# Two steps' results in one 8 MB store, with q and k transposed in place (rotary embedding and q·k scores, float32)

## The chip, the cores and the metric

One core of a Trainium2 chip. The metric is the device time of one execution in microseconds, the median of several runs. Each group of runs stood beside fresh runs of the kernel before on the same chip; the groups were on different chips, so small differences between groups are rough. DVE is VectorE, ACT ScalarE, PE TensorE; SP is the engine whose queue issues nearly all DMA transfers. A transfer is cut into packets, which 16 DMA engines carry: a 4 MB store is 128 packets of 32 KB, eight for each engine. It has landed when its completion is signalled. The *span* is the time of the profiled execution.

## The reference

```python
# q, k: (16, 512, 16, 64) float32; cos, sin: (512, 32)
q_rot = concat([q1*cos - q2*sin, q1*sin + q2*cos])     # k the same
scores = einsum('bshd,bthd->bsht', q_rot, k_rot)       # (16, 512, 16, 512) float32
```

Inputs are 67 MB, the result 268 MB. So the kernel lives from its DMA queue.

## The kernel before

A batch of 512 rows is four *steps* of 128 rows; there are 64 steps. In each one VectorE rotates q and k, TensorE transposes them (into PSUM) and multiplies, ScalarE copies the scores from PSUM into a stage tile of 32 KB per partition, and SP stores the tile. The parts that matter, abridged:

```python
kt_pool = tile_pool(name="kt", bufs=2);  qt_pool = tile_pool(name="qt", bufs=2)   # transposed copies
stage_pool = tile_pool(name="stage", bufs=3)                                      # 3 x 32 KB per partition
o_v = out.rearrange("b (p c) h t -> b c p h t", c=C)
...
def load(which, b):                       # a batch of q or k: 2 MB in one DMA
    ...
def store(i, st):                         # one step: 4 MB
    if i < NST - 1:
        nc.sync.dma_start(o_v[i // C, i % C], st)
        return
    h = H - 2                             # the last step: 14 heads on all DMA engines,
    nc.sync.dma_start(o[:, :h], st[:, :h])
    nc.sync.dma_start(o[:116, h:], st[:116, h:])   # two heads in a split
    nc.sync.dma_start(o[116:, h:], st[116:, h:])
...
# batch 0 (steps 0 to 3) stores 1 MB at a time; k of batch 3 is loaded after step 3
# steps 4 to 63: scores, store(i), rotation and transposes for later steps, loads
```

## Time and profile before

| | before |
|---|---|
| time | 800.53 us (3 runs); 800.99 with a fourth |
| busy: PE, ACT, DVE | 87%, 70%, 68% |
| data queue | 98.6% of the span |
| moved | 335.55 MB on this queue, 336.17 MB on all; 421 GB/s over the span |

The profile is read from the DMA row down. A queue that is full nearly all the time is the bound, and the waits of engines matter only if they leave it empty. Its lines are in the prediction below.

### The profile page before, as it was taken

What the parts mean: (1) busy time and instruction counts of PE and PEld (TensorE: products, weight loads), DVE (VectorE), ACT (ScalarE), POOL (GpSimd) and SP (SyncE); (2) the same over time, 40 slices, a digit from 0 to 9 for tenths busy, and PEclk for the clock granted to TensorE, in tenths of its full rate; (3) what the DMA queues carried; (4) which work ended last, traced back from release to release, by engine and by line L of the source; (5) the groups of instructions that cost most, each with busy time, mean ns of one, the idle gap of its engine ahead of it and who ended that gap; (6) DMA issues with size and microseconds to landing.
All of it is one profiled execution on the core that took longest, in us unless ns stands there. A gap on an engine that the chain in (4) does not pass through costs nothing.

```text
span 799.0 us, 7715 instructions
## 1 busy us (share of the span) xinstructions
PE 691.3 (87%) x3072; PEld 299.3 (37%) x3072; DVE 544.6 (68%) x516; ACT 561.2 (70%) x647; POOL 0.7 (0%) x6
## 2 busy tenths in 40 slices
PE   4989998997979979799797997979979799799970
PEld 2444443343434334343343443424434343344420
DVE  6999987676866768577585775857758478585300
ACT  3888886775857758577585775757757677578870
POOL 0000000000000000000000000000000000000000
PEclk9999999898998989889898898988989899899995
DMA  9999999999999999999999999999999999998995
GB/s 355 422 424 424 432 427 433 425 435 427 421 437 426 439 427 430 433 431 430 431 428 433 434 428 429 433 438 420 418 426 434 435 415 418 426 440 375 422 439 231
DMA packets 17844, 336.17 MB, mean 421 GB/s; under 512 B 1808, under 2 KB 3088, under 8 KB 4240
## 3 DMA queue, kind: packets, MB, share of 16 engines
q1 hardware_dynamic: 17520, 335.55, 98.6%
q8 instruction: 24, 0.39, 0.2%
q10 hardware_dynamic: 288, 0.13, 0.1%
q14 instruction: 12, 0.10, 0.0%
HBM read 67.24 MB, written 268.44 MB: 420 GB/s over the span
## 4 chain that ended last, share of the span: by engine, by line
DMA 50%; PE 40%; ACT 4%; DVE 3%; issue 1%; ACTq 0%; SPq 0%; DVEq 0%
DMA out_dram<-st 47%; PE ps L166 30%; PE bank L127 10%; ACT st L173 4%; DMA q_sb<-in_q_dram 2%; DVE part L106 1%; DMA early<-in_k_dram 1%; DVE q_sb L107 0%; DVE k_sb L107 0%; DVE k_sb L111 0%; DVE q_sb L111 0%; DVE early L107 0%; DVE kT_t L142 0%; ACTq L281 0%; DVE early L111 0%
## 5 line engine op out<-in xcount | busy, mean ns | idle before, releaser
L173 ACT COPY st<-ps 128x1024 f32<-128x1024 f32 x512 | 494.7, 1018 | 203.7 <-DMA out_dram<-st 105.6
L166 PE MATMUL ps<-kT_t,qT_t 64*128 64x512 f32 x2048 | 548.9, 654 | 71.0 <-ACT st L173 70.9
L166 PEld LDWEIGHTS ps<-kT_t,qT_t 64*128 64x128 f32 x2048 | 185.0, 197 | 261.7 <-issue 144.6
L142 DVE COPY qT_t<-bank 128x512 f32<-128x512 f32 x118 | 81.6, 691 | 203.8 <-PE bank L127 203.8
L127 PEld LDWEIGHTS bank<-ident,q_sb 128*128 128x128 f32 x480 | 55.6, 152 | 102.5 <-issue 99.1
L127 PE MATMUL bank<-ident,q_sb 128*128 128x128 f32 x480 | 86.9, 308 | 0.9 <-PE ps L166 0.9
L127 PEld LDWEIGHTS bank<-ident,k_sb 128*128 128x128 f32 x480 | 50.5, 141 | 95.4 <-issue 38.7
L127 PE MATMUL bank<-ident,k_sb 128*128 128x128 f32 x480 | 78.7, 287 | 1.6 <-DVE qT_t L142 1.2
L142 ACT COPY kT_t<-bank 128x512 f32<-128x512 f32 x122 | 72.5, 599 | 6.4 <-PE bank L127 6.4
L107 DVE TENSOR_TENSOR q_sb<-q_sb,cos_t 128x1024 f32<-128x1024 f32 x60 | 73.5, 1226 | 2.1
L111 DVE TENSOR_TENSOR k_sb<-k_sb,part 128x1024 f32<-128x1024 f32 x60 | 73.5, 1225 | 2.1
L107 DVE TENSOR_TENSOR k_sb<-k_sb,cos_t 128x1024 f32<-128x1024 f32 x60 | 73.5, 1225 | 2.0
L106 DVE TENSOR_TENSOR part<-q_sb,ss_t 128x1024 f32<-128x1024 f32 x60 | 73.5, 1225 | 2.0
L106 DVE TENSOR_TENSOR part<-k_sb,ss_t 128x1024 f32<-128x1024 f32 x60 | 73.0, 1216 | 0.1
L111 DVE TENSOR_TENSOR q_sb<-q_sb,part 128x1024 f32<-128x1024 f32 x60 | 73.0, 1216 | 0.0
L127 PE MATMUL bank<-ident,early 128*128 128x128 f32 x64 | 10.5, 316 | 12.5 <-DVE early L111 10.6
L127 PEld LDWEIGHTS bank<-ident,early 128*128 128x128 f32 x64 | 8.3, 161 | 17.5 <-issue 13.4
L106 DVE TENSOR_TENSOR part<-early,ss_t 128x1024 f32<-128x1024 f32 x8 | 9.8, 1223 | 5.9 <-DMA early<-in_k_dram 5.8
L111 DVE TENSOR_TENSOR early<-early,part 128x512 f32<-128x512 f32 x16 | 10.3, 687 | 0.2
L107 DVE TENSOR_TENSOR early<-early,cos_t 128x1024 f32<-128x1024 f32 x8 | 9.8, 1225 | 0.3
L142 ACT COPY qT_t<-bank 128x512 f32<-128x512 f32 x10 | 5.7, 617 | 3.2 <-PE bank L127 3.2
L142 DVE COPY kT_t<-bank 128x512 f32<-128x512 f32 x6 | 4.1, 685 | 0.3 <-PE bank L127 0.3
(9 smaller groups left out, 2.8 us busy)
## 6 DMA issues: line engine op xcount, KB each, us to landing
out_dram<-st SPq DMA_DIRECT2D x59, 4096.0 KB, 23.9
k_sb<-in_k_dram SPq DMA_DIRECT2D x15, 2048.0 KB, 26.9
q_sb<-in_q_dram SPq DMA_DIRECT2D x15, 2048.0 KB, 29.9
out_dram<-st SPq DMA_DIRECT2D x16, 1024.0 KB, 14.3
out_dram<-st SPq DMA_DIRECT2D x1, 3584.0 KB, 20.4
early<-in_k_dram SPq DMA_DIRECT2D x1, 1536.0 KB, 8.9
early<-in_q_dram SPq DMA_DIRECT2D x1, 1536.0 KB, 12.1
early<-in_k_dram SPq DMA_DIRECT2D x1, 512.0 KB
```

What stands on the lines that cost most here:

```text
L106: nc.vector.tensor_tensor(pv, xs, ss, op=mult)
L107: nc.vector.tensor_tensor(xc, xc, cs, op=mult)
L111: nc.vector.tensor_tensor(y, y, z, op=add)
L127: nc.tensor.transpose(bank[:, x, :], src, ident)
L142: copy(out=dst, in_=src)
L166: nc.tensor.matmul(out=po, lhsT=lhs[64 * r : 64 * r + 64, :], rhs=rh, start=True, stop=True)
L173: nc.scalar.copy(out=so, in_=si)
```

## The change

The transposed blocks are written back over their source in the input tiles, so the tiles for transposed q and k go. The memory makes two stage tiles of 64 KB per partition, each for two steps, whose result goes out in one store of 8 MB with 64 KB of contiguous memory per partition. q is loaded in 1 MB pieces, k of batch 2 is loaded at the very start instead of in step 0, and k of batch 3 moves from the end of step 3 into step 2.

```diff
-    kt_pool = ctx.enter_context(tc.tile_pool(name="kt", bufs=2))
-    qt_pool = ctx.enter_context(tc.tile_pool(name="qt", bufs=2))
-    stage_pool = ctx.enter_context(tc.tile_pool(name="stage", bufs=3))
+    stage_pool = ctx.enter_context(tc.tile_pool(name="stage", bufs=2))
...
+    tile_a, tile_b = new_pair(), new_pair()          # [P, 2, H, S]
+    halves = {0: tile_a[:, 0], 1: tile_a[:, 1], 2: tile_b[:, 0], 3: tile_a[:, 0]}
+    def store(i, st):
+        b, c = divmod(i, C)
+        if i == NST - 1:
+            last(o_v[b, :, c], st)
+        elif i == NST - 2:
+            nc.sync.dma_start(o_v[b, :, c], st)
+        elif i % 2 == 1:
+            nc.sync.dma_start(o_v[b, :, c - 1 : c + 1], pairs[i // 2])
...
+    SLOTS = {"k": C, "q": QS}                        # QS = 2: q in 1 MB loads
+    BUFS = {"k": 3, "q": 3}
...
-        copy(out=dst, in_=src)
+        copy(out=x, in_=bank)                        # transposed in place
...
-            if i % C == C - 2:
-                load("q", i // C + 2)
-            elif i % C == C - 1:
-                load("k", i // C + 3)
+            store(i, st)
+            if (i + 1) % QS == 0:
+                load("q", i // QS + BUFS["q"])
+            if c == C - 1:
+                load("k", b + BUFS["k"])
```

More of the change, by code (lines that the diff above doesn't have):

```diff
@@ L31 @@
     G = H // C
+    QS = C // 2
     const_pool = ctx.enter_context(tc.tile_pool(name="const", bufs=1))
@@ L46 @@
     }
-    o_v = out.rearrange("b (p c) h t -> b c p h t", c=C)
+    o_v = out.rearrange("b (p c) h t -> b p c h t", c=C)
     ident = const_pool.tile([P, P], fp32, name="ident")
@@ L53, with last, new_pair, stage @@
     ss_v = ss_t.rearrange("p c x j -> p c (x j)")
-    st_first = [stage_pool.tile([P, H, S], fp32, tag="stage", name="st") for _ in range(2)]
-    early = stage_pool.tile([P, 2 * C * H * D], fp32, tag="stage", name="early")
+    def last(o, st):
+        h = H - 2
+        nc.sync.dma_start(o[:, :h], st[:, :h])
+        nc.sync.dma_start(o[:116, h:], st[:116, h:])
+        nc.sync.dma_start(o[116:, h:], st[116:, h:])
+    def new_pair():
+        return stage_pool.tile([P, 2, H, S], fp32, tag="stage", name="st")
+    tile_a, tile_b = new_pair(), new_pair()
+    pairs = {C // 2: tile_b}
+    halves = {0: tile_a[:, 0], 1: tile_a[:, 1], 2: tile_b[:, 0], 3: tile_a[:, 0]}
+    def stage(i):
+        if i < C:
+            return halves[i]
+        if i // 2 not in pairs:
+            pairs[i // 2] = new_pair()
+        return pairs[i // 2][:, i % 2]
+    def store(i, st):
[6 more added lines that the diff above has]
+            nc.sync.dma_start(o_v[b, :, c - 1 : c + 1], pairs[i // 2])
+    early = tile_b[:, 1].rearrange("p h t -> p (h t)")
     units = {}
@@ L69, in load_units, with load, rope @@
             units[which, (head + h) // G] = t[:, :, D * h : D * (h + G)]
-    batches = {}
-    def load(which, b):
+    tiles = {}
+    SLOTS = {"k": C, "q": QS}
+    BUFS = {"k": 3, "q": 3}
+    def load(which, m):
+        n = SLOTS[which]
+        b, c = divmod(m * n, C)
         if b >= B:
             return
-        t = in_pool.tile([P, C, H * D], fp32, tag=which + "_in", name=which + "_sb")
-        batches[which, b] = t
-        nc.sync.dma_start(t.rearrange("p c (h d) -> p c h d", h=H), dram[which][b])
-    def rope(which, n):
+        t = in_pool.tile(
+            [P, n, H * D], fp32, tag=which + "_in", bufs=BUFS[which], name=which + "_sb"
+        )
+        for x in range(n):
+            tiles[which, m * n + x] = t, x
+        nc.sync.dma_start(
+            t.rearrange("p c (h d) -> p c h d", h=H), dram[which][b, :, c : c + n]
+        )
+    def rope(which, n, count=1):
         part = part_pool.tile([P, H * D], fp32, tag="part", name="part")
@@ L86, in rope @@
             x = units[which, n]
-            sv, k1, k2 = "p c (g j) -> p c g j", {"j": HD}, {"j": D}
+            part = part[:, : H * D]
             cs = cos_t.unsqueeze(2).to_broadcast((P, C, 2 * G, HD))
             ss = ss_v.unsqueeze(2).to_broadcast((P, C, G, D))
-            pv = part.rearrange("p (c g j) -> p c g j", c=C, j=D)
             x5 = x.rearrange("p c (h x j) -> p c h x j", x=2, j=HD)
@@ L93, in rope @@
             adds = [(x5[:, :, :, y], p5[:, :, :, 1 - y]) for y in range(2)]
+            nc_ = C
         else:
-            x = batches[which, n // C][:, n % C]
-            sv, k1, k2 = "p (g j) -> p g j", {"j": HD}, {"j": D}
-            cs = cos_t[:, n % C].unsqueeze(1).to_broadcast((P, 2 * H, HD))
-            ss = ss_v[:, n % C].unsqueeze(1).to_broadcast((P, H, D))
-            pv = part.rearrange(sv, **k2)
-            x4 = x.rearrange("p (h x j) -> p h x j", x=2, j=HD)
-            swapped = bass.AP(part.tensor, part.offset + HD, [part.ap[0], (D, H), (-HD, 2), (1, HD)])
+            t, y = tiles[which, n]
+            x = t[:, y : y + count]
+            part = part[:, : count * H * D]
+            c = n % C
+            cs = cos_t[:, c : c + count].unsqueeze(2).to_broadcast((P, count, 2 * H, HD))
+            ss = ss_v[:, c : c + count].unsqueeze(2).to_broadcast((P, count, H, D))
+            x4 = x.rearrange("p c (h x j) -> p (c h) x j", x=2, j=HD)
+            swapped = bass.AP(
+                part.tensor, part.offset + HD, [part.ap[0], (D, count * H), (-HD, 2), (1, HD)]
+            )
             adds = [(x4, swapped)]
-        xs, xc = x.rearrange(sv, **k2), x.rearrange(sv, **k1)
+            nc_ = count
+        pv = part.rearrange("p (c g j) -> p c g j", c=nc_, j=D)
+        xs = x.rearrange("p c (g j) -> p c g j", j=D)
+        xc = x.rearrange("p c (g j) -> p c g j", j=HD)
         def products():
@@ L113, in rope, with block, q_block @@
         return [products, sums]
-    kT = {}
-    qT = {}
+    def block(which, n, hp):
+        if n == 0:
+            return units[which, hp // 2][:, :, P * (hp % 2) : P * (hp % 2 + 1)]
+        return tiles[which, C * n][0][:, :, P * hp : P * (hp + 1)]
+    def q_block(n, c, hp):
+        if n == 0:
+            return block("q", 0, hp)[:, c]
+        t, y = tiles["q", C * n + c]
+        return t[:, y, P * hp : P * (hp + 1)]
     def transposed(which, n, g, copy):
         bank = ps_t_pool.tile([P, 4, P], fp32, tag="ps_t", name="bank")
-        for x in range(4):
-            if n < C:
-                src = units[which, n][:, x, P * g : P * (g + 1)]
-            else:
-                src = batches[which, n // C][:, n % C, P * (4 * g + x) : P * (4 * g + x + 1)]
-            nc.tensor.transpose(bank[:, x, :], src, ident)
-        src = bank
-        if which == "q":
-            if n not in qT:
-                qT[n] = qt_pool.tile([P, HP, P], fp32, tag="qT", name="qT_t")
-            dst = qT[n][:, 4 * g : 4 * g + 4, :]
-        else:
-            b = n // C
-            if b not in kT:
-                kT[b] = kt_pool.tile([P, HP, S], fp32, tag="kT", name="kT_t")
-            if n < C:
-                dst = kT[b][:, 2 * n + g].rearrange("p (t c) -> p t c", c=C)
-                src = bank.rearrange("p c t -> p t c")
-            else:
-                dst = kT[b][:, 4 * g : 4 * g + 4, P * (n % C) : P * (n % C + 1)]
-        copy(out=dst, in_=src)
@@ L144, in store @@
-    def store(i, st):
-        o = o_v[i // C, i % C]
-        if i < NST - 1:
-            nc.sync.dma_start(o, st)
-            return
-        h = H - 2
-        nc.sync.dma_start(o[:, :h], st[:, :h])
-        nc.sync.dma_start(o[:116, h:], st[:116, h:])
-        nc.sync.dma_start(o[116:, h:], st[116:, h:])
-    def scores(i, p, st):
-        ps = ps_s_pool.tile([P, 2, S], fp32, tag="ps_s", name="ps")
-        b = i // C
-        if b == 0:
-            c, hp = divmod(p, 2)
-            lhs, rhs = qT[i][:, C * hp + c], kT[0][:, 2 * i + hp]
-        else:
-            lhs, rhs = qT[i][:, p], kT[b][:, p]
+        if n < C:
+            x = block(which, 0, 2 * n + g)
+        else:
+            t, y = tiles[which, n]
+            x = t[:, y, 4 * P * g : 4 * P * (g + 1)].rearrange("p (g e) -> p g e", e=P)
@@ L164, in scores @@
+        for y in range(4):
+            nc.tensor.transpose(bank[:, y, :], x[:, y], ident)
+        copy(out=x, in_=bank)
+    def scores(lhs, rhs, so):
+        ps = ps_s_pool.tile([P, 2, S], fp32, tag="ps_s", name="ps")
         for r in range(2):
-            po, rh = ps[:, r, :], rhs[64 * r : 64 * r + 64, :]
             nc.tensor.matmul(
-                out=po, lhsT=lhs[64 * r : 64 * r + 64, :], rhs=rh, start=True, stop=True
-            )
-        so, si = st[:, 2 * p : 2 * p + 2, :], ps
@@ L170, in scores @@
-        if b > 0:
-            so = so.rearrange("s r (t c) -> s r t c", c=C)
-            si = si.rearrange("s r (c t) -> s r t c", c=C)
-        nc.scalar.copy(out=so, in_=si)
-        if b == 0 and p % 2 == 1:
-            c = p // 2
-            nc.sync.dma_start(o_v[0, c, :, G * i : G * (i + 1)], st[:, G * c : G * (c + 1)])
-        elif b > 0 and p == HP - 1:
-            store(i, st)
+                out=ps[:, r, :].rearrange("s (c t) -> s c t", c=C),
+                lhsT=lhs[64 * r : 64 * r + 64],
@@ L180, in tr_act @@
+                rhs=rhs[64 * r : 64 * r + 64],
+                start=True,
+                stop=True,
+            )
+        nc.scalar.copy(
+            out=so.rearrange("s r (t c) -> s r t c", c=C),
+            in_=ps.rearrange("s r (c t) -> s r t c", c=C),
+        )
     def tr_act(which, n):
@@ L194 @@
         load("k", 1)
-        load("q", 1)
+        load("q", C // QS)
+        load("k", 2)
         make_identity(nc, ident)
@@ L204 @@
         for i in range(C):
-            st = st_first[i] if i < 2 else stage_pool.tile([P, H, S], fp32, tag="stage", name="st")
+            st = stage(i)
             if i < C - 1:
@@ L212 @@
             for p in range(HP):
-                scores(i, p, st)
+                c, hp = divmod(p, 2)
+                hp += 2 * i
+                scores(q_block(0, c, hp), block("k", 0, hp), st[:, 2 * p : 2 * p + 2])
                 if p in (0, 1) and i > 0:
@@ L217 @@
                     transposed("k", C + i - 1, p, nc.vector.tensor_copy)
-                if p == 3 and i < 2:
-                    load("kq"[i], 2)
+                if p % 2 == 1:
+                    nc.sync.dma_start(
+                        o_v[0, :, c, G * i : G * (i + 1)], st[:, G * c : G * (c + 1)]
+                    )
+                if p == 3:
+                    if i == 0:
+                        load("q", 3)
+                    elif i == 1:
+                        load("q", 4)
+                    elif i == 2:
+                        load("k", 3)
                 if p in (2, 6):
@@ L225 @@
             run(dve)
-        load("k", 3)
         for i in range(C, NST):
+            b, c = divmod(i, C)
             tr = {}
@@ L239 @@
                 dve += rope("k", i + 1 + C)
-            st = stage_pool.tile([P, H, S], fp32, tag="stage", name="st")
+            st = stage(i)
             for p in range(HP):
-                scores(i, p, st)
+                scores(q_block(b, c, p), block("k", b, p), st[:, 2 * p : 2 * p + 2])
                 if p not in tr:
```

## The prediction

> **What bounds the kernel now.** I read the page first, from the slices down.
>
> ```profile
> PEclk9999999898998989889898898988989899899995
> DMA  9999999999999999999999999999999999998995
> ...
> q1 hardware_dynamic: 17520, 335.55, 98.6%
> ...
> out_dram<-st SPq DMA_DIRECT2D x59, 4096.0 KB, 23.9
> k_sb<-in_k_dram SPq DMA_DIRECT2D x15, 2048.0 KB, 26.9
> q_sb<-in_q_dram SPq DMA_DIRECT2D x15, 2048.0 KB, 29.9
> out_dram<-st SPq DMA_DIRECT2D x16, 1024.0 KB, 14.3
> ```
>
> The DMA row is at 9 in all but the last slices, and the one queue that carries the data has packets on its 16 engines for 98.6% of the 799.0 us span. PE (87%), ACT (70%) and DVE (68%) have idle time. A 4 MB store takes some 10 us of the queue but 23.9 us to land: it lies behind others. Next, the table of waits and the chain of one store in order of time:
>
> ```profile
> ACT st L173 <- DMA out_dram<-st: 105.6, 28, 6.0
> ```
> ```profile
> 162.28 26.96 DMA out_dram<-st
> ...
> 189.35 1.02 ACT st L173
> ...
> 209.74 1.02 ACT st L173
> ...
> 210.78 28.27 DMA out_dram<-st
> ```
>
> ACT waits 28 times for a stage tile to be written out, then two steps are computed and stored, and their store is again the wait. From release (189.35) to the second store's issue (210.78) is 21.4 us; the next time round, 239.15 to 261.28, it is 22.1. Undisturbed steps follow each other at 10.02 us. One batch (4 steps) costs the queue about 49 us and the engines 40. So time is the queue's work plus whatever time the queue stands empty. Where could it stand empty? The queue's own timeline at the start, and the shares of stretches:
>
> ```profile
> 35.34 27.44 SPq L176 DMA_DIRECT2D out_dram<-st  x10
> 62.88 1.03 SPq L79 DMA_DIRECT2D k_sb<-in_k_dram  x1
> 73.85 20.37 SPq L147 DMA_DIRECT2D out_dram<-st  x3
> ```
> ```profile
> 20.00:76.00 56.00, 52.62 (x267) 24.68 (x267) 54.61 (x55) 46.65 (x58) 0.00 (x0) 1.00 1.01 425
> 76.00:114.00 38.00, 38.00 (x186) 16.78 (x182) 34.55 (x33) 33.01 (x39) 0.00 (x0) 1.00 1.01 429
> ...
> 760.00:800.00 40.00, 14.24 (x56) 5.65 (x56) 0.69 (x1) 15.12 (x16) 0.00 (x0) 0.74 0.76 322
> ```
>
> Step 3's last store is issued at 62.8, step 4's at 73.85 and the next at about 83.9 and 93.9. The DMA share (last column but one) is 1 from 20 us on, so even here the queue never runs dry; the loss is at the very end (0.76).
>
> The packet records of the same trace give the queue's prices. Median (mean) time of a packet on its engine: 8 KB 309 (311) ns, 16 KB 611 (628), 32 KB 1213 (1218). That is a line of 27.2 GB/s per engine plus 9 ns per packet. With 8 packets per engine: a 4 MB store 8 x 1.218 = 9.75 us, a 2 MB load 8 x 0.628 = 5.02, a 1 MB store 8 x 0.311 = 2.49. The early loads (1 and 3 KB packets) occupy the queue from 2.2 to 13.5 us.
>
> **What the Trainium skill says.**
> - "DMA: Bandwidth & Descriptors", section "Where 436 GB/s comes from": 16 ports give 435.2 GB/s. The trace agrees: 27.2 x 16 = 435. As 429 is already moved in mid-run, 335.55 MB at the ceiling (an estimate: 771 us) leaves little to win.
> - The same page, "Why small descriptors are slow (HBM only)", names a fixed overhead of a few cycles per packet. The 9 ns above are of that kind, and at 32 KB they are 0.7%.
> - The same page, "Anatomy of one DMA": completion costs about 2 us, mostly the wait for the write's receipt. It agrees: by the prices above step 0's stores end at 13.5 + 10.0 (k, q of batch 1) + 9.96 + 5.02 (k of batch 2 in between) = 38.5 us, and ACT, which waits for them at step 2, starts at 40.52. I use 2.0.
> - "TensorE: Matmul & The Clock Gate", "What's actually happening": an idle window of about 3.4 us halves the clock. The page's PEclk dips and the 22.1 beside 21.4 us are this; it is in the 21.4 to 22.1 that I use.
>
> **The change, part by part.**
> 1. *Transposes in place.* Same instructions: 6 VectorE products and sums of 1.22 us a step, 16 transposes, 4 copies of 0.6 to 0.7 us. Nothing is saved on any engine; only the two transposed buffers go. Worth 0.
> 2. *8 MB stores, 64 KB per partition and packet* (batches 1 to 15). Halves 7,552 packets of 32 KB, less those of the last steps: about 3,700 x 9 ns / 16 engines = -2.1 us, if the hardware takes 64 KB as one packet.
> 3. *q loads of 1 MB instead of 2 MB.* 30 loads x 128 packets of 8 KB for 15 x 128 of 16 KB: +1,920 x 9 ns / 16 = +1.1 us. A 1 MB load is about 2.55 us.
> 4. *Two stages of two steps for three of one.* Steady state: write S for the start of a pair's store on the queue. Two pairs cost the queue 2 x 19.42 (8 x 2.428 us) + 2 x 2.55 + 5.02 = 48.95 us. A stage is free at S + 19.42 + 2.0, filled 21.4 to 22.1 later, and its store reaches the engines about 1.5 us after issue (first issue 0.73, first packets 2.2): S + 44.3 to 45.0. So 3.9 to 4.6 us of slack, and the queue does not run dry. The q load for the step after next lands 2.55 us after the release; VectorE's delayed copy then ends about 5.7 us after it, before TensorE wants that bank (about 7 us after: 196.38 against 189.35). Worth 0. When k loads have ended (after step 51) two pairs cost 43.9, against 44.3 to 45.0: gaps of about +1 us in all.
> 5. *The first pair.* Here it goes wrong. Step 4 (the first of batch 1) no longer stores itself: nothing is issued until step 5 is done. I also checked the order of issues: behind step 3's stores there is no load, since k of batch 3 moved ahead into step 2 and the next q load comes after the pair's store. Queue work up to there: 13.5 + 5.02 (k) + 2.55 (q) + 5.02 (k) + 16 x 2.49 + 2 x 2.55 (q) + 5.02 (k) = 76.0 us. Step 5 ends when it did, at 83.9: VectorE runs without idle time from 6 to 68 us and sets the pace of the first steps, then steps come at 10.02. The waits for stage parts don't bind (the built program waits part by part; step 2's third and fourth stores land at about 65.7 and 68.2, and step 4 writes there after 67 and 70). So the queue is empty from 76.0 to 83.9 + 1.5 = 85.4: **+9.4 us**. Afterwards: the 8 MB store and a q load keep it until 107.4, the next pair is issued at 103.9; no second gap.
> 6. *The end.* The same split of the last step, fed by a queue that is full. In the window 728 to 732 us most engines already idled before, but some engine was still at older packets: packet records show one engine some 8 us behind the others at the end (others end at about 789 to 795, it ends at 797.6), and it sets the time. That dip was therefore free, and removing it gains nothing. At 76 us that engine is only about 1 us behind, so -0.5 of the gap.
>
> Sum: 0 - 2.1 + 1.1 + 1.0 + 9.4 - 0.5 = +8.9, so 800.5 + 8.9 = **809.4 us**.
>
> **The rivals.**
> - *Fewer, larger stores make the queue faster.* For it: it is the bound. Against: 9 ns per packet is all there is, and the measured line already meets the ceiling. If right and without the gap: about 797 to 799.
> - *Two stages starve the queue in every pair.* For it: slack falls to about 4 us, and a slow engine, half clock or a late q load eat it. Two microseconds lost in each of 28 pairs would make 866, half a microsecond 823. Against: the measured 21.4 to 22.1 already contain waits of 4.2 to 5.5 us and the halved clock.
> - *No gap at the start*, if steps 2 to 5 run earlier than before (step 2's wait of 2.38 us for a stage goes away) or the queue is later than I add up: about 801. VectorE's full occupancy there speaks against it.
> - *A 64 KB packet is split in two:* +2.1, about 811.5.
>
> **Range and chances.** The gap is good to about 3 us either way, the packet prices to 2; the steady state can only add. That makes 804 to 816 for 8 in 10. Faster than 784.5 would need a queue above the port ceiling: 0.02. Slower than 816.5 needs a steady gap of over 0.25 us per pair on top: 0.13. Within 2%: 0.85.
>
> **What would show it.** The start's slices 3 and 4 (60 to 100 us) should have a DMA share below 9 and the queue's timeline its first 8 MB store at about 84, with no issue between about 63 and that; the share of 76 to 85 near 0. In mid-run the DMA share stays 1.00 at 429 to 431 GB/s, ACT's wait for stores comes about once a pair, as long as 4 us, and the packets under the data queue fall by about 1,800. I am wrong if the first pair's store goes out before 78, if a stretch of a pair in mid-run shows a share under 0.97, or if packets of 64 KB take other than about 2.42 us.

## The result, and the profile after

| | before | after |
|---|---|---|
| median | 800.99 us (4 runs) | 811.65 us (4 runs, 811.36 to 813.21) |
| ratio, 95% interval | | 1.0137 (1.0122 to 1.0153) |
| data queue | 98.6% | 97.4% |
| packets on it | 17,520 | 15,504 |

The change cost 11 us, 1.4%.

The page after, first the DMA row of the 40 slices, then the queue and the q loads:

```profile
DMA  9997899999999999999999999999999999979997
q1 hardware_dynamic: 15504, 335.55, 97.4%
q_sb<-in_q_dram SPq DMA_DIRECT2D x30, 1024.0 KB, 30.8
```

The 7 in the fourth slice (60.9 to 81.1 us) is new, and so is the 8 after it. The queue's own timeline after shows why (start, duration and count of issues):

```profile
47.86 15.56 SPq L245 DMA_DIRECT2D out_dram<-st  x6
84.45 0.33 SPq L84 DMA_DIRECT2D out_dram<-st  x1
84.89 0.63 SPq L117 DMA_DIRECT2D q_sb<-in_q_dram  x1
104.49 0.33 SPq L84 DMA_DIRECT2D out_dram<-st  x1
```

Step 3's last part is issued by 63.4 (47.86 + 15.56), and then nothing until the first pair's store at 84.45. Before, step 4's store was issued at 73.85. Busy times by stretch after (columns: stretch, length, busy time of PE, its weight loads, DVE, ACT and POOL with counts, clock, DMA share, GB/s):

```profile
76.00:85.00 9.00, 9.00 (x44) 3.71 (x40) 8.85 (x9) 7.72 (x10) 0.00 (x0) 1.00 0.03 9
114.00:400.00 286.00, 250.62 (x1130) 108.09 (x1132) 197.18 (x189) 204.24 (x234) 0.00 (x0) 0.93 1.00 429
400.00:700.00 300.00, 256.17 (x1156) 110.24 (x1152) 201.08 (x192) 209.71 (x240) 0.00 (x0) 0.93 1.00 426
700.00:760.00 60.00, 54.00 (x244) 23.48 (x246) 38.95 (x39) 46.33 (x52) 0.00 (x0) 0.94 0.93 390
```

From 76 to 85 us PE and DVE work with hardly a pause (9.00 and 8.85 of 9 us) and ACT for 7.72, while the queue stands at 0.03. Afterwards it is full until 700 us; from there to 760 us it stands at 0.93 (0.96 before). Adding up the packet records, which is good to about half a microsecond, the 16 DMA engines are idle for 9.6 us on average between 60 and 100 us (0.0 before), and 1.1 us between 400 and 700 (0.2 before). A 64 KB packet is one packet, median 2418 ns.

The waits after, and the chain, tell a different story at first sight:

```profile
DVE part L152 <- DMA q_sb<-in_q_dram: 208.3, 27, 10.6
ACT st L198 <- DMA out_dram<-st: 110.3, 27, 7.5
```
```profile
DMA q_sb<-in_q_dram 50%; PE ps L191 23%; PE bank L183 8%; DVE part L152 4%; DMA out_dram<-st 3%; DVE q_sb L153 2%; ACT st L198 2%; DVE q_sb L184 1%; DVE st L157 1%; DVE k_sb L157 1%; DVE k_sb L153 1%; DVE st L153 1%; DMA sin_t<-in_sin_dram 1%; DVE k_sb L184 0%; DVE q_sb L157 0%
```

VectorE now waits 27 times for a q load, and half the chain runs through these loads. Whether that costs anything had to be tried.

### The profile page after: what moved, and what is told of

Read it like the earlier page. It is cut to its first block, busy times and chain, and to the rows that moved or that the text cites. A ratio compares the mean times of both kernels' runs of the same rounds, so it can differ in the third digit from the quotient of the medians.

```text
span 811.4 us, 7751 instructions
## 1 busy us (share of the span) xinstructions
PE 677.9 (84%) x3072; PEld 295.2 (36%) x3072; DVE 535.4 (66%) x516; ACT 562.3 (69%) x647; POOL 0.7 (0%) x6
## 3 DMA queue, kind: packets, MB, share of 16 engines
q1 hardware_dynamic: 15504, 335.55, 97.4%
## 4 chain that ended last, share of the span: by engine, by line
DMA 53%; PE 31%; DVE 10%; ACT 2%; issue 1%; ACTq 0%; DVEq 0%
DMA q_sb<-in_q_dram 50%; PE ps L191 23%; PE bank L183 8%; DVE part L152 4%; DMA out_dram<-st 3%; DVE q_sb L153 2%; ACT st L198 2%; DVE q_sb L184 1%; DVE st L157 1%; DVE k_sb L157 1%; DVE k_sb L153 1%; DVE st L153 1%; DMA sin_t<-in_sin_dram 1%; DVE k_sb L184 0%; DVE q_sb L157 0%
## 5 line engine op out<-in xcount | busy, mean ns | idle before, releaser
L191 PE MATMUL ps<-k_sb,q_sb 64*128 64x512 f32 x1920 | 502.4, 640 | 80.0 <-ACT st L198 79.2
L191 PEld LDWEIGHTS ps<-k_sb,q_sb 64*128 64x128 f32 x1920 | 170.5, 194 | 251.9 <-issue 129.0
L184 DVE COPY q_sb<-bank 128x512 f32<-128x512 f32 x118 | 80.7, 684 | 16.0 <-PE bank L183 15.6
L184 ACT COPY k_sb<-bank 128x512 f32<-128x512 f32 x114 | 67.7, 595 | 8.3 <-PE bank L183 8.2
L191 PE MATMUL ps<-st 64*128 64x512 f32 x128 | 33.3, 643 | 0.0
L183 PE MATMUL bank<-ident,st 128*128 128x128 f32 x64 | 10.5, 316 | 12.5 <-DVE st L157 10.6
L191 PEld LDWEIGHTS ps<-st 64*128 64x128 f32 x128 | 11.6, 197 | 11.9 <-issue 8.3
L184 ACT COPY st<-bank 128x512 f32<-128x512 f32 x16 | 9.0, 608 | 8.5 <-PE bank L183 8.5
L152 DVE TENSOR_TENSOR part<-st,ss_t 128x1024 f32<-128x1024 f32 x8 | 9.8, 1222 | 6.0 <-ACT ss_t L222 5.8
L157 DVE TENSOR_TENSOR st<-st,part 128x512 f32<-128x512 f32 x16 | 10.3, 687 | 0.2
```

The lines of the kernel that those rows point to most:

```text
L152: nc.vector.tensor_tensor(pv, xs, ss, op=mult)
L157: nc.vector.tensor_tensor(y, y, z, op=add)
L183: nc.tensor.transpose(bank[:, y, :], x[:, y], ident)
L184: copy(out=x, in_=bank)
L191: nc.tensor.matmul(out=ps[:, r, :].rearrange("s (c t) -> s c t", c=C), lhsT=lhs[64 * r : 64 * r + 64], rhs=rhs[64 * r : 64 * r + 64], star ...
```

## The experiments

The theories, as the expectations name them. **A**: the loss is the time in which the queue is empty at the start, since a store of two steps needs more work ahead of it in the queue than there is. **B**: only the first pair is special. **C**: the loss is in mid-run, in VectorE's late q loads or in having two stages for three. All experiments gave correct results.

### One pair stored step by step

```diff
-        elif i == NST - 2:
+        elif i == NST - 2 or i < C + 2:
```

> The changed kernel with steps 4 and 5 (the first pair) stored one by one, each when it is done. Theory A (the 9.5 us in which the queue is empty from 76 to 85 us is the loss, because the queue has too little ahead of it for a store of two steps): step 4's store reaches the engines at 75.4, the queue goes on to 76.0 + 9.75 + 9.75 + 2.55 = 98.2, but the store of steps 6 and 7 is issued only at 104.5 and starts at 106.0, so the gap moves there and is 7.8 us instead of 9.5. The time gains only 1.4 us: about 810. Theory B (only the first pair is special, a cost of starting): the gap goes and the time is about 802. Theory C (the loss lies in the middle of the run, in the wait of VectorE for the q loads or in the two stages): within 1 us of the changed kernel, and no different where the gap is.

Measured: 809.43 us (before, on the same chip, 800.96; ratio 1.010). The gap did move. Stretches of this run:

```profile
76.00:85.00 9.00, 9.00 (x46) 3.94 (x42) 8.83 (x9) 7.92 (x10) 0.00 (x0) 1.00 1.01 434
97.00:108.00 11.00, 11.00 (x56) 5.15 (x56) 8.85 (x10) 9.67 (x12) 0.00 (x0) 1.00 0.56 235
```

The queue is full where it was empty, and half empty 20 us later (idle time from 60 to 400 us: 6.6 us). So B falls: what matters is how much work lies in the queue when the first pair is due. A step gives the queue 9.75 us of store and some 2.5 of loads for 10.02 us of computing, so it gains only about 2.2 us a step on the engines.

### Two pairs stored step by step

```diff
-        elif i == NST - 2:
+        elif i == NST - 2 or i < C + 4:
```

> The changed kernel with the first two pairs (steps 4 to 7) stored step by step. Theory A: step 6's store is issued at 94.4, before the queue's 98.2, step 7's at 104.5 before 107.9, then loads to 125.2; the store of steps 8 and 9 is ready at 125.5. No gap over 1 us; the first full pair in mid-run starts at 125.5 instead of 134.4, so 8.9 us are won: about 802.7. Theory C: no gain beyond 2 us.

Measured: 804.96 us (ratio 1.0039). The idle time from 60 to 400 us is 0.4 us. The mean falls by 7.1 us against the changed kernel's (from another group of runs), which is most of the loss, though less than the 8.9 expected. C, which allowed a gain of 2 us at most, can't be the whole story.

### Two 4 MB stores for each pair: a miss of mine that told something

```diff
-            nc.sync.dma_start(o_v[b, :, c - 1 : c + 1], pairs[i // 2])
+            for y in range(2):
+                nc.sync.dma_start(o_v[b, :, c - 1 + y], pairs[i // 2][:, y])
```

> The changed kernel with each pair written by two 4 MB stores, both issued at the end of the pair: same times of issue, packets of 32 KB instead of 64 KB. By the medians (2 x 1213 against 2418 ns) the queue's work grows by 3,712 x 8 ns / 16 = 1.9 us, so about 813.5. If large packets are slower than they look (the mean of 64 KB packets is 2441 ns, 23 over the median; of 32 KB in the kernel before 1218, 5 over), it is 1 us faster, about 810.5. Rival (the 8 MB store itself costs something, for instance in the time to landing): faster by several us.

Measured: 802.79 us (ratio 1.0014, interval 0.9985 to 1.0042). This looked like the rival's victory, but the queue's timeline of this run shows that the stores weren't issued together:

```profile
75.38 10.30 SPq L85 DMA_DIRECT2D out_dram<-st  x2
85.78 0.37 SPq L118 DMA_DIRECT2D q_sb<-in_q_dram  x1
95.36 10.35 SPq L85 DMA_DIRECT2D out_dram<-st  x2
```

The first of the two left at 75.4 and the second 10 us later. At the first of them SP waited only for the step that this store reads; that the program names it after step 5 did not hold it back. The run is therefore "the changed kernel with all stores by step", and as that it is worth more than what I meant: pair tiles, transposes in place and 1 MB q loads stay, only the holding back of each first step goes, and nearly all of the loss goes with it. VectorE's wait for q loads stays too, 191.8 us in 26 waits:

```profile
DVE part L153 <- DMA q_sb<-in_q_dram: 191.8, 26, 10.9
```

That wait, and with it 47% of this run's chain, is thus nearly free: the whole run is only 1.3 us (means) behind the kernel before. It lies beside a full queue.

### The kernel before with one store held back: an edit that did nothing

```diff
+            if i == C:
+                held.append(st); return
+            if i == C + 1:
+                store(C, held.pop())
             store(i, st)
```

> The kernel before, with nothing changed but that step 4's store is held back and issued together with step 5's. Theory A: the queue runs dry at 78.3 (here k of batch 3 is behind step 3's stores) and goes on at 84.4 + 1.5 = 85.9: a gap of 7.6 us that nothing gives back, so about 808. Theory C: no more than 1 us slower than the kernel before, as the three stages stay and all later stores are single.

Measured: 801.21 us (ratio 0.9992). For the same reason as above the store still went out at 74.55, when its own step was done, so this run tests nothing but the noise:

```profile
74.55 20.37 SPq L148 DMA_DIRECT2D out_dram<-st  x3
```

### Held back in earnest, in both kernels

Both were repeated with the order turned round: SP stands at the later step's store first, and the earlier step's behind it really waits. The changed kernel with two 4 MB stores:

```diff
+            for y in (1, 0):
+                nc.sync.dma_start(o_v[b, :, c - 1 + y], pairs[i // 2][:, y])
```

> The changed kernel with each pair as two 4 MB stores, step 2's first in the queue, so that both really wait for the end of the pair (in the earlier run of two stores the first went out as soon as its own step was done, which made it a test of stores by step). Only the packet is changed, 32 KB for 64 KB. If 64 KB packets cost or save nothing: within 2 us of the changed kernel's 811.6, with the queue empty from 76 to 85 as there. By the medians 1.9 us slower, by the means 1 us faster. If the size of the packet were what made the changed kernel slow (rival): about 803, as in the run of two stores that were not held.

Measured: 814.12 us (ratio 1.0169). The timeline has both stores from 84.92 on:

```profile
84.92 1.05 SPq L85 DMA_DIRECT2D out_dram<-st  x2
```

The mean is 2.3 us over the changed kernel's 811.97 (from another group of runs), against 1.9 expected from the medians. So 64 KB packets save about 2 us (the two ratios with their intervals leave some 1 to 4), and holding back the first step of each pair costs 11.4 us (814.25 less 802.83, the means of this run and of the run by step).

The kernel before with step 4's store held behind step 5's:

```diff
             store(i, st)
+            if i == C + 1:
+                store(C, held.pop())
```

> The kernel before with step 4's store really held: it stands in the queue behind step 5's. Theory A': the queue is empty from 78.3 to 85.9, 7.6 us on the average engine, but the end of the kernel is set by the one DMA engine that lags, and that is already 2.9 us behind at this point (its packets of that load end 2.9 us after the others'), so it idles 4.7 us only: about 805.5. Theory A without the lag: 808.5. Theory C (the first pair is harmless, the cost is in mid-run): 801.

Measured: 809.01 us (before 800.79; ratio 1.0106, interval 1.0091 to 1.0121). In its timeline and its stretches:

```profile
84.94 10.35 SPq L148 DMA_DIRECT2D out_dram<-st  x3
```
```profile
76.00:85.00 9.00, 9.00 (x46) 4.01 (x44) 8.86 (x9) 7.67 (x10) 0.00 (x0) 1.00 0.24 100
```

One store moved by 10 us, everything else as before, and 8.3 us are lost (means). The idle time from 60 to 100 us is 7.4 us. This is the gap by itself, put into a kernel that had none, and nothing gives it back later. Theory A holds; the refinement A', that the lagging engine feels less of it, does not.

### q loads ahead of the stores

```diff
-            store(i, st)
             if (i + 1) % QS == 0:
                 load("q", i // QS + BUFS["q"])
+            store(i, st)
```

> The changed kernel with each pair's q load put into the queue ahead of the pair's store. q then lands a store (19.4 us) earlier, and VectorE's 208 us of waits for q loads all but vanish. Theory A: they lie beside the queue's work, which is the same, so the time stays within 2 us of 811.6 (it may be up to 2 slower: the queue has 2.55 us less behind a store that must land, so the slack falls to 1.3 to 2.1 us). Rival C (the late q load, which the chain of waits shows as half the span, delays the steps and so costs time): faster by several us.

Measured: 828.24 us (ratio 1.0337), 16 us slower than the changed kernel. VectorE's wait for q loads did vanish from its list, and the time grew. So the half of C that blames the late q loads is wrong twice over, and I was wrong about the slack. Stretches of this run and of the changed kernel:

```profile
428.00:436.00 8.00, 8.00 (x42) 3.49 (x38) 7.21 (x7) 6.69 (x8) 0.00 (x0) 1.00 0.87 329
```
```profile
428.00:436.00 8.00, 7.22 (x35) 3.23 (x36) 5.83 (x6) 6.93 (x9) 0.00 (x0) 1.00 1.00 433
```

In this run the queue has run out of other work at every second pair, from about 230 us on. By the packet records the q load then starts 1.0 to 1.8 us after its issue (3.3 to 4.7 at the pairs between), and its 8 KB packets take 394 to 498 ns on average, where those of the pairs between take 309 to 324. Over the run such longer packets come to 12 us more than in the changed kernel, and idle time from 100 to 760 us to 4 us more: together the 16 us. A load that meets engines with nothing else to do was the dearer part.

The slack that I took for 1.3 us at least was not there. In the changed kernel a pair's store finds 5 to 6 us of other work before it in the queue at 129 to 200 us, but 0.8 us, which is the bare start of a store, at 427, 526, 625 and 724 us. At the same time one DMA engine falls behind: its last packet of a k load ends 2.3 us after the 112th of the load's 128 at 185 us, and 5.1 us after it at 429. The stage waits for this engine: of the store issued at 178.61, 112 packets had ended at 203.2, the last one at 206.18, the completion came at 206.53 and ACT went on at 206.63. That the lag ate the slack fits these records; no run takes the lag away, so it is not shown.

### One engine sets the end

The kernel before should then gain if that engine gets less to do at the end.

```diff
-        h = H - 2
+        h = H - 6
-        nc.sync.dma_start(o[:116, h:], st[:116, h:])
-        nc.sync.dma_start(o[116:, h:], st[116:, h:])
+        nc.sync.dma_start(o[:119, h:], st[:119, h:])
+        nc.sync.dma_start(o[119:, h:], st[119:, h:])
```

> The kernel before, with the last step's last six heads (instead of two) moved off most DMA engines: 119 partitions in one store, which the hardware spreads over 7 engines, and 9 in another. If one slow DMA engine outside those 7 sets the end (797.5, the others at 788.5), it has 4 x 8 x 2 KB = 64 KB or 2.4 us less to do and the end comes 2 to 2.4 us earlier: about 798.7. The 7 engines end at about 788.5 - 2.4 + 17 x 0.45 = 793.8, in its shadow. If the end is set by anything else: no gain, or 3 us slower.

Measured: 808.32 us (before 800.79; ratio 1.0095). A miss, and the end of the trace says why:

```profile
787.00:795.00 8.00, 0.00 (x0) 0.00 (x0) 0.00 (x0) 0.00 (x0) 0.00 (x0) 0.50 0.44 164
797.00:803.00 6.00, 0.00 (x0) 0.00 (x0) 0.00 (x0) 0.00 (x0) 0.00 (x0) 0.50 0.07 29
```

A share of 0.44 is 7 engines of 16: six that write the split store and one still at older packets. And 0.07 is one engine: its packets of 20 KB, the first 10 heads, end at 796.1 us, then it writes 18 packets of 12 KB until 804.5 (17 of the 119-partition store, one of the other). The laggard is one of the seven, and I had given it more instead of less: 18 x 0.47 = 8.4 us. The 2.4 us less before that came to 1.4 in this trace (796.1 for 797.5), and the times are 7.5 us apart. The arithmetic went wrong by the choice of engines; that one engine sets the end is shown by it all the same. The split with 116 partitions, which the kernel has, does avoid it: there the laggard writes a single 4 KB packet after its 28 KB ones.

### Pairs only where there was slack

```diff
-        elif i == NST - 2:
+        elif i == NST - 2 or i < C + 4 or i >= NST // 2:
```

> The run with the first two pairs stored step by step, and from step 32 on stored step by step again: pairs of 64 KB packets stay only for steps 8 to 31, where a pair's store was issued 4 to 6 us before the queue reached it. Theory: of what that run is still behind the kernel before (805.0 against 801.0), the idle time of the queue after 400 us (1.8 us up to 700 us, 2.7 to 760 us, on the average engine) comes of the pairs in the second half, where a lagging DMA engine has used up the slack. Then the time falls by 2 to 3 us less 1 us for the smaller packets: 802 to 803.5, near the run with all steps stored singly (802.8). If the pairs in the second half cost nothing: 806.

Measured: 804.78 us (ratio 1.0040), no better than with pairs to the end (804.96). The idle time did go where I wanted it, from 4.5 to 0.8 us between 400 and 760. It came back after that. Stretches of this run, then of the run with pairs to the end:

```profile
700.00:760.00 60.00, 57.16 (x266) 24.54 (x264) 38.74 (x39) 46.56 (x53) 0.00 (x0) 0.99 0.99 418
760.00:790.00 30.00, 14.61 (x56) 5.78 (x56) 0.69 (x1) 14.95 (x16) 0.00 (x0) 0.78 0.92 393
790.00:794.00 4.00, 0.00 (x0) 0.00 (x0) 0.00 (x0) 0.00 (x0) 0.00 (x0) 0.50 0.71 272
```
```profile
700.00:760.00 60.00, 55.27 (x262) 23.64 (x258) 36.92 (x37) 46.14 (x52) 0.00 (x0) 1.00 0.96 406
760.00:790.00 30.00, 14.64 (x56) 5.78 (x56) 0.69 (x1) 14.95 (x16) 0.00 (x0) 0.74 0.99 429
790.00:794.00 4.00, 0.00 (x0) 0.00 (x0) 0.00 (x0) 0.00 (x0) 0.00 (x0) 0.50 1.05 452
```

Here one engine ends last, its last 28 KB packet 8.5 us after the 112th of that store's 128. With pairs to the end it is only 3.4 us behind in the same way; there the others had idled 4.5 us in mid-run, where here they idled 0.8. So moving the wait bought nothing, or at most the 1.1 us that the smaller packets of this run cost (1,920 x 9 ns / 16). The average share of busy engines doesn't show this, the slowest engine does.

### q in 1 MB loads in the kernel before

```diff
+        n = C if which == "k" else C // 2
+        for c in range(0, C, n):
+            nc.sync.dma_start(tv[:, c : c + n], dram[which][b, :, c : c + n])
```

> The kernel before with each 2 MB load of q made as two loads of 1 MB, issued together: 8 KB packets instead of 16 KB, as in the changed kernel, and nothing else. By the medians 15 x 128 more packets cost 9 ns each on 16 engines: +1.1 us; by the means of the changed kernel's trace up to +1.7. So about 802.2. This would be part of the 2 to 4 us by which the versions without the gap are still behind. If it shows nothing (800.5 to 801.3), the rest lies elsewhere.

Measured: 802.15 us against 801.08 (ratio 1.0011, interval 0.9997 to 1.0025). The size is that expected, but it is not clear of the noise.

No run beat the kernel before. A fourth q buffer, to have q earlier without a change in the order, doesn't fit: such a kernel does not build, as 121.3 KB per partition are left for stages that need 128.

## Why the prediction was right, point by point

811.65 us lies in the range of 804 to 816, 2.2 us over the 809.4.

1. **Transposes in place: 0.** Right. The run by step has them and is 1.3 us (means) behind the kernel before, about what the small q loads cost alone.
2. **64 KB packets: -2.1.** Right: one packet of 2418 ns in the records, and -2.3 against the same kernel with 32 KB packets, if roughly.
3. **1 MB q loads: +1.1.** +1.1 in the medians, not clear of the noise.
4. **Steady state: slack of 3.9 to 4.6 us, cost 0.** The step that failed, though little of the error is its. The sum treated the 16 DMA engines as one. Slack was there at first and gone by some 430 us, while one engine lagged; the run with q first, which takes 2.55 us of it, lost 16 us. Two readings hid this. The 2.0 us taken for completion were mostly the late engine: step 0's last packets end at 38.5 us on the middle engine but at about 39.8 on the last, and in the changed kernel's first pairs completion comes 0.34 to 0.48 us after the last packet. And against the rival of starving pairs, the waits of 4.2 to 5.5 us are not contained in the 21.4 to 22.1 us: they end where these begin. The sum's +1.0 for the pairs after the k loads is of the right size as idle time (700 to 760 us: 4.4 us for 2.6 before), but what it cost is not shown. VectorE's late q, which I called harmless, was harmless.
5. **The first pair: +9.4.** Right, and the main term: empty from 76.0 to 85.4 by the sum, from about 76 (the last engine 78.1) to 85.3 by the packets. The store was issued half a microsecond later than I took and reached the engines 0.8 us after issue, not 1.5. Taking the gap away won 7.1 us; putting one of 7.4 us into the kernel before cost 8.3.
6. **The end: dips there are free, and -0.5 for the lag.** The first is borne out by the run with pairs only in mid-run. The -0.5 is not: the kernel before lost the whole of its gap. Nor was the engine only 1 us behind at 76 us: its last packet of the k load there ends 2.9 us after the 112th. And in the changed kernel it no longer ends last: its 28 KB packets end at 808.0, and the four engines with the 116-partition store at 810.0.

Of the prediction's signs, the first store at 84.45 with nothing before it, the share of 0.03 and the 64 KB packets of 2.42 us came as told, and seven stretches of 24 or 25 us between 427 and 675 us stand at 0.98 to 1.02. ACT's waits came 27 times, but up to 7.5 us long instead of 4. The packets fell by 2,016, not 1,800: the sum left out 224 records of 4 bytes, 16 for each transfer.

What stays open: holding back the first step of each pair cost 11.4 us, of which the idle queue at the start is 9.1 (9.9 less 0.8 us in the two runs). About 2 us more come from the pairs in mid-run or at the end, so the half of C that blames two stages is not refuted; the run with two pairs split, 2.0 us (means) behind the run by step in spite of its larger packets, points the same way. The traces show one candidate, the split of the very last store. In those with pairs to the end (the changed kernel, one and two pairs split, stores held) its 116-partition part ends 2.0 to 2.2 us after the lagging engine's 28 KB packets; in those with single stores at the end (the kernel before, the run by step, pairs only in the first half) the lagging engine is last, and only one packet of 0.16 us follows. The means of the 32 KB packets are also a little longer (5.4 us in all over the medians with stores held, 2.9 by step). No run takes this apart. Nor is it known why one DMA engine lags.

## What to carry to other kernels

A queue that is the bound is never to be left empty, and a larger store must be paid for with work already in the queue: count what lies ahead of it at the moment at which the first store of the new size is due, above all at the start, where little has piled up. Fewer, larger packets are worth only the overhead of a packet, here 9 ns of 1213. A wait that fills half of the chain may still be free: see whether the bound resource is full beside it before you cure it. And to hold a store back it is not enough to write it later: it left at 75.4 us when nothing unready stood ahead of it in SP's program, and at 84.9 when a later step's store did.

## What the Trainium skill lacked or had wrong

- "DMA: Bandwidth & Descriptors", section "Latency and other measured facts", says that engines 7 and 15 are usually the slow ones and, as a best guess, puts it down to SWDGE. Here all but the 0.13 MB of cos and sin went by the sync queue, and one engine fell 8 us behind by 700 us. It was among the engines that got the 119-partition store, and not among those that got the 116-partition one. By the same page's rule for k ("Why a DMA increments its semaphore by 16 and not by 1": the lowest-numbered k, here 7 and 4), that makes it engine 4, 5 or 6, if it is the same engine in the different runs; the trace doesn't number engines.
- The same section gives HWDGE about 600 ns to the first byte. A store into an empty queue took 0.8 us from issue to its first packet (84.45 to about 85.3).
- That page has no figure for completion on the sync queue; the section from which the prediction took its 2.0 us is about transfers issued from GpSimd. Here completion came 0.34 to 0.48 us after the last packet (the changed kernel's first five pairs, such as 105.88 to 106.24 us).
- That page has no price for large packets on the sync queue: medians of 309, 611, 1213 and 2418 ns for 8, 16, 32 and 64 KB, or 27.2 GB/s and about 9 ns a packet. 64 KB goes as one packet.
- No page tells how a load into an idle queue differs: in the run with q first, 8 KB packets took 394 to 498 ns on average there, against 309 to 324 behind other work.
- No page warns that a full average hides one late engine: in the kernel before, the DMA share is 1.00 between 400 and 700 us, and one engine is 8 us behind at its end.
